# Remainder columns stored through a shared output slot, and a lone quad interleaved with the next pair, in a one-core QKV projection

## The chip, the cores and the metric

The kernel runs on one core of one Trainium2 chip. The metric is the device time of one execution in microseconds (us). The core has five engines with an instruction queue each: TensorE (PE in the profile; its weight loads are PEld), VectorE (DVE), ScalarE (ACT), GpSimd (POOL) and SyncE (SP), which here only issues DMAs. ACT issues some DMAs as well.

## The reference: what is computed

```
x: (16, 512, 768) float32      w_qkv: (768, 2304) float32
qkv = matmul(x, w_qkv)
q, k, v = qkv[..., :768], qkv[..., 768:1536], qkv[..., 1536:]
return stack([q, k, v], axis=0)
```

It is one product of an 8192 x 768 matrix with a 768 x 2304 matrix; its columns are stored as three matrices.

## The kernel before

**Tiles.** The 8192 rows are worked on in 32 pairs of 128 rows, `p` = 0 to 31. The 2304 columns are two blocks of 1024, called `q` = 0 and 1, and a remainder of 256 columns between them. One *quad* is one pair of rows with one block of columns: four output tiles c11, c12, c21, c22 of 128 x 512, held in one SBUF tile `o` (pool `o_pool`, five slots) and stored by two DMAs of 768 KB and 256 KB (`store_quad`, L259/L260 for block 0, L263/L264 for block 1).

**The product.** From pair 2 on a quad is computed with seven products in place of eight (the Strassen-Winograd scheme): `do(u, n)` for n = 1 to 7. Each product is three matmuls of 128x128 by 128x512 (L218). do(1) and do(2) use the bf16 copy `xb` of x and the bf16 block `b1`; the others use sums of x (`s`, made by `sums_x`) and sums of w (`t1` to `t4`, made by `sum_w`). Several products add into one PSUM bank, which is copied out in between: do(1) to bank u.x, copied to c11 by ACT (L232); do(2) to bank u.z, added to c11 by DVE (L236); do(6) adds to u.x, which ACT copies to c12 (L239); do(5) starts bank u.y; do(7) adds to u.x; do(4) adds to u.x, copied to c21 (L249); do(3) adds to u.y, which DVE adds to c12 (L252). A product that adds to a bank has to wait for the copy that reads it. [...]

**The remainder.** `rem(p)` makes the 256 remainder columns of a pair: twelve bf16 matmuls (L268), a copy by ACT (L278) and one store of 256 KB (L279).

**The first three pairs.** While weights are still being loaded, pairs 0 and 1 are computed plainly in bf16 (`block`, L405, copies L395). The order of the program, which is also each engine's order, is: block 0's first half for pairs 0 and 1; `rem(0)` and `rem(1)`, whose stores ACT issues; block 0's second half; the first products of pair 2's first quad, `alone(u, ...)` at L479, with the copies of the last block results (`late[2]`, `late[3]`) and `rem(2)` put between its steps; the casts of the second block's weights on ACT (`cast_js`, L483); block 1's first half for pairs 0 and 1; pair 2's do(4) and the store of its first quad (L495, L496); block 1's second half; pair 2's second quad, `alone(u, {})` at L506.

**The loop.** From pair 3 on, `two(a, b, early)` works both quads of a pair in the order of L283 to L300. `early` transposes the next pair's x on DVE (L134), casts it and sums it on POOL (L176, L185 to L189), and issues the load of the pair after that, half by SP and half by ACT (L126). For pair 3 alone, `early` first ends pair 2's second quad with do(4) and its store.

**What sets the order.** The schedule is manual: every engine executes its instructions in the order of the program, and a wait of one holds all behind it on that engine. SP's and ACT's DMAs are queues of their own (q1 and q10 in the profile). DMAs share eight completion semaphores in turn, so an issue can wait until the DMA eight places earlier has landed. A new `o` tile takes the slot that has been free for longest, and its first writer, the c11 copy at L232 or the copy at L395, waits until the stores of the slot's last tile have landed. The first `o` slot is taken by the staged remainder weights (`str`).

Of the kernel before, what the change touches and what calls it, by code (L numbers as in the profile page):

```python
# [10 lines left out]
def kernel(  # L11
# [20 lines left out]
    nc = tc.nc  # L32
    P = 128
    G = 32
    B, T, H = x.shape
# [3 lines left out]
    KT = K // P  # L39
    KH = KT // 2  # L40
    KC = K // 4
    NP = M // (2 * P)
    CB = 512
    REM = N3 - 4 * CB
    Q_OFF = (0, 2 * CB + REM)
    R_OFF = 2 * CB
    fp32 = mybir.dt.float32
    f32r = mybir.dt.float32r
    bf16 = mybir.dt.bfloat16
    ident = mybir.ActivationFunctionType.Identity  # L50
# [11 lines left out]
    o_pool = ctx.enter_context(tc.tile_pool(name="o", bufs=5))  # L62
    st_pool = ctx.enter_context(tc.tile_pool(name="st", bufs=4))
    or_pool = ctx.enter_context(tc.tile_pool(name="or", bufs=2))
# [13 lines left out]
    b1 = [w_pool.tile([P, KT, CB], bf16, name=f"b1_{q}") for q in range(2)]  # L78
# [12 lines left out]
    stage = {}  # L91
# [108 lines left out]
    def quad(p, q):  # L200
        u = Quad()
        u.p, u.q = p, q
        u.o = o_pool.tile([P, 2, 2 * CB], fp32, name="o", tag="o")
        u.x = u.y = u.z = None
        return u

    def product(u, n, ps, start):
        t1, t2, t3, t4 = ts[u.q]
        if n <= 2:
            h = (n - 1) * KH  # L210
            lhs = [xb[u.p][:, h + j, :P] for j in range(KH)]
            rhs = [b1[u.q][:, h + j, :] for j in range(KH)]
        else:
            k, t = {3: (4, b22[u.q][:]), 4: (0, t4), 5: (1, t1), 6: (2, t2), 7: (3, t3)}[n]
            lhs = [sr[u.p][:, k, j, :] for j in range(KH)]
            rhs = [t[:, j, :] for j in range(KH)]
        for j in range(KH):
            nc.tensor.matmul(  # L218
                ps[:], lhs[j], rhs[j],
                start=(start and j == 0), stop=(j == KH - 1), skip_group_check=True,  # L220
            )

    def bank():
        return ps_pool.tile([P, CB], fp32, name="ps")

    def do(u, n):
        c11, c12 = u.o[:, 0, :CB], u.o[:, 0, CB:]
        c21, c22 = u.o[:, 1, :CB], u.o[:, 1, CB:]
        if n == 1:
            u.x = bank()  # L230
            product(u, 1, u.x, True)
            nc.scalar.activation(c11, u.x[:], ident)  # L232
        elif n == 2:
            u.z = bank()
            product(u, 2, u.z, True)
            nc.vector.tensor_tensor(c11, c11, u.z[:], op=add)  # L236
        elif n == 6:
            product(u, 6, u.x, False)
            nc.scalar.activation(c12, u.x[:], ident)  # L239
        elif n == 5:  # L240
            u.y = bank()
            product(u, 5, u.y, True)
        elif n == 7:
            product(u, 7, u.x, False)
            nc.scalar.activation(c22, u.x[:], ident)  # L245
            nc.vector.tensor_tensor(c22, c22, u.y[:], op=add)  # L246
        elif n == 4:
            product(u, 4, u.x, False)
            nc.scalar.activation(c21, u.x[:], ident)  # L249
        elif n == 3:  # L250
            product(u, 3, u.y, False)
            nc.vector.tensor_tensor(c12, c12, u.y[:], op=add)  # L252

    def rows_of(s, p, lo, hi):
        return out_flat[s, p * 2 * P:(p + 1) * 2 * P, lo:hi].rearrange("(r m) n -> m r n", m=P)

    def store_quad(u):
        if u.q == 0:
            nc.sync.dma_start(rows_of(0, u.p, 0, H), u.o[:, :, :H])  # L259
            nc.sync.dma_start(rows_of(1, u.p, 0, 2 * CB - H), u.o[:, :, H:])  # L260
        else:
            part = 2 * H - Q_OFF[1]
            nc.sync.dma_start(rows_of(1, u.p, H - part, H), u.o[:, :, :part])  # L263
            nc.sync.dma_start(rows_of(2, u.p, 0, H), u.o[:, :, part:])  # L264

    def rem_row(p, r, ps):
        for j in range(KT):
            nc.tensor.matmul(  # L268
                ps, xb[p][:, j, r * P:(r + 1) * P], w_rem[j // KH][:, j % KH, :],
                start=(j == 0), stop=(j == KT - 1), skip_group_check=True,  # L270
            )

    def rem(p, eng=nc.sync):
        ps = ps_pool.tile([P, 2, REM], fp32, name="ps")
        for r in range(2):
            rem_row(p, r, ps[:, r, :])
        o = or_pool.tile([P, 2, REM], fp32, name="orem")
        nc.scalar.activation(o[:], ps[:], ident)  # L278
        eng.dma_start(rows_of(1, p, R_OFF - H, R_OFF - H + REM), o[:])  # L279

    def two(a, b, early):

        do(a, 1)  # L283
        do(b, 1)
        early()
        rem(a.p)
        do(a, 2)
        do(b, 2)
        do(a, 6)
        do(b, 6)  # L290
        do(a, 5)
        do(a, 7)
        do(b, 5)
        do(b, 7)
        do(a, 4)
        do(a, 3)
        store_quad(a)
        do(b, 4)
        do(b, 3)
        store_quad(b)  # L300

    def store_cols(u, r, lo, hi, eng):

        c = Q_OFF[u.q] + lo
        end = Q_OFF[u.q] + hi
        while c < end:
            n = min(end, (c // H + 1) * H)
            row = (2 * u.p + r) * P
            eng.dma_start(  # L309
                out_flat[c // H, row:row + P, c % H:c % H + n - c],  # L310
                u.o[:, r, c - Q_OFF[u.q]:n - Q_OFF[u.q]],
            )
            c = n

    def last(a, b):

        p = a.p

        def rem_stored(r):
            ps = bank()  # L320
            rem_row(p, r, ps[:, :REM])
            o = or_pool.tile([P, 2, REM], fp32, name="orem")
            nc.scalar.activation(o[:, 0, :], ps[:, :REM], ident)  # L323
            row = (2 * p + r) * P
            nc.scalar.dma_start(out_flat[1, row:row + P, R_OFF - H:R_OFF - H + REM], o[:, 0, :])  # L325

        do(a, 1)
        do(b, 1)
        do(a, 2)
        do(a, 6)  # L330
        do(b, 2)
        do(b, 6)
        for u in (a, b):
            store_cols(u, 0, 0, CB, nc.sync)
        for u in (a, b):
            do(u, 5)
            do(u, 7)
            store_cols(u, 1, CB, 2 * CB, nc.sync)
        do(a, 4)
        store_cols(a, 1, 0, CB, nc.scalar)  # L340
        rem_stored(0)
        do(b, 4)
        store_cols(b, 1, 0, CB, nc.scalar)
        for u in (a, b):
            do(u, 3)
            store_cols(u, 0, CB, 2 * CB, nc.sync)
        rem_stored(1)


    ND = 2  # L350
# [18 lines left out]
        for _ in range(n):  # L369
            nc.tensor.matmul(ps[:], zero[:, :P], zero[:], start=True, stop=True)  # L370

    act, dve = nc.scalar, nc.vector

    def cast(q, h, c, w, eng):

        dst = w[:, h * KH:(h + 1) * KH, :]
        if eng is act:
            eng.activation(dst, stage[q, h, c], ident)
        else:
            eng.tensor_copy(out=dst, in_=stage[q, h, c])  # L380
# [35 lines left out]
    def halves(tiles):  # L416
        return [(range(h * KH, (h + 1) * KH), tiles) for h in range(2)]

    def alone(u, after):


        c22 = u.o[:, 1, CB:]
        for n in (1, 2):
            do(u, n)
            after.get(n, lambda: None)()
        do(u, 6)
        do(u, 5)
        act.activation(c22, u.y[:], ident)  # L428
        after.get(5, lambda: None)()
        product(u, 7, u.x, False)  # L430
        dve.tensor_tensor(c22, c22, u.x[:], op=add)
        do(u, 3)

    def ahead(p):
        transpose(p)
        round_x(p)
        sums_x(p)
# [17 lines left out]

    for f in block(0, 0, b1[0], singles):
        f()
    rem(0, act)
    rem(1, act)
    cast(0, 0, 1, bt0, dve)  # L460
    cast(0, 1, 1, bt0, act)
    sum_w(0, 1)
# [4 lines left out]
    late = block(0, 1, bt0, halves(range(4)))  # L467
# [7 lines left out]
    sum_w(0, 3)  # L475
    sums[3](dve)
    sums[4](dve)
    u = quad(2, 0)
    alone(u, {1: late[2], 2: lambda: rem(2), 5: late[3]})  # L479

    def cast_js(q, c, w):
        for j in range(KT):
            act.activation(w[:, j, :], stage[q, j // KH, c][:, j % KH, :], ident)  # L483

    cast_js(1, 0, b1[1])
    bt1 = bt_pool.tile([P, KT, CB], bf16, name="bt")
    cast_js(1, 1, bt1)
    sum_w(0, 4)
    load_x(4, nc.sync)
    t_1 = [tq_pool.tile([P, 2, KH, CB], f32r, name=f"t_1{n}", tag="tq") for n in range(2)]  # L490
# [12 lines left out]
    for f in block(1, 1, bt1, halves(range(4))):  # L503
        f()
    u = quad(2, 1)
    alone(u, {})  # L506

    for p in range(ND + 1, NP):
        def early():
            if p == ND + 1:  # L510
                do(u, 4)
                store_quad(u)
            if p + 1 < NP:
                ahead(p + 1)
            if p + 2 < NP:
                load_x(p + 2, nc.scalar)

        if p < NP - 1:
            two(quad(p, 0), quad(p, 1), early)
        else:  # L520
            last(quad(p, 0), quad(p, 1))


# [28 lines left out]
```

## Time and profile before

| what | value |
|---|---|
| median of three runs | 362.6 us (362.59, 362.60, 363.93) |
| the profiled execution: time | 363.91 us |
| its span, first to last instruction | 362.1 us |
| PE matmul, busy | 352.1 us (97%) |
| PE weight load / DVE / ACT / POOL, busy | 251.2 / 227.7 / 188.7 / 174.3 us |
| moved by DMA | 108.08 MB, 298 GB/s over the span |
| same from 5 to 45 us, in stretches of 5 us | 312 to 406 GB/s, engines' share 1.04 to 1.09 |

The time of an execution holds 1.8 us that lie outside the span. Each of the sixteen DMA engines can have packets of more than one transfer in work, so their share can be over 1. A line of the timeline gives the start of a group of like instructions, its duration, engine, source line, operation, what it writes and reads, how many there are, and in brackets how long the engine had been idle before, and who ended that. A matmul of 128x512 starts every 0.216 us in bf16 and every 0.227 us in the wider type when nothing holds it up, though each is shown with some 0.38 us since they are pipelined. Some records of matmuls are missing.

### The profile page before, as it was taken

The page shows a single profiled execution, that of the slowest core. Times are in us where ns is not written, and L with a number is a line of the kernel's source. Part 1 is how long each engine was busy: PE and PEld are TensorE (multiplying, and loading weights), DVE is VectorE, ACT ScalarE, POOL GpSimd, SP SyncE. Part 2 cuts the span into 40 slices and gives each one's busy share as a digit, 9 for nine tenths or more (in the row PEclk, how much of TensorE's full clock was granted, in tenths as well). Part 3 has the DMA queues.
Part 4 walks back from the last instruction along what each step waited for, and adds up shares of the span by engine and source line. Part 5 has one row for each costly group of instructions (what it writes and reads, how often), then busy time and mean ns, then how long its engine had stood idle before and what let it go on. Part 6 is the DMA issues. An engine that isn't in the chain of part 4 may idle for free.

```text
span 362.1 us, 5215 instructions
## 1 busy us (share of the span) xinstructions
PE 352.1 (97%) x1747; PEld 251.2 (69%) x1779; DVE 227.7 (63%) x240; ACT 188.7 (52%) x317; POOL 174.3 (48%) x181
## 2 busy tenths in 40 slices
PE   8979999999999999999999999999999999999995
PEld 3545577777777777777777777777777777777763
DVE  3679866755656755566765566675565676556643
ACT  4579745455454554454545454545445455545452
POOL 0000773456654446654446664445665444666420
PEclk9999999999999999999999999999999999999999
DMA  7999988989999989899999999898999998989766
GB/s 297 375 376 358 369 285 291 269 286 293 316 306 290 291 277 292 287 319 296 300 272 296 274 325 313 282 276 295 279 308 309 291 289 279 293 281 323 288 248 245
DMA packets 81433, 108.08 MB, mean 298 GB/s; under 512 B 4864, under 2 KB 61440, under 8 KB 81408
## 3 DMA queue, kind: packets, MB, share of 16 engines
q1 hardware_dynamic: 65456, 95.83, 81.2%
q10 hardware_dynamic: 15952, 11.93, 10.0%
q8 instruction: 14, 0.23, 0.3%
q14 instruction: 11, 0.09, 0.1%
HBM read 32.24 MB, written 75.50 MB: 298 GB/s over the span
## 4 chain that ended last, share of the span: by engine, by line
PE 87%; DMA 7%; ACT 4%; issue 1%; ACTq 0%; DVE 0%
PE ps L218 76%; PE ps L268 11%; DMA xin<-in_x_dram 4%; DMA str<-in_w_qkv_dram 2%; DMA out_dram<-o 1%; ACT bt L483 1%; ACT b L483 1%; ACT o L395 1%; ACT o L249 0%; DVE xf L134 0%; ACTq L309 0%; ACT xb L470 0%; ACT orem L323 0%; ACT o L232 0%; ACTq L325 0%
## 5 line engine op out<-in xcount | busy, mean ns | idle before, releaser
L218 PE MATMUL ps<-t,s 128*128 128x512 f32 x720 | 181.1, 399 | 0.2
L218 PEld LDWEIGHTS ps<-t,s 128*128 128x128 f32 x720 | 134.9, 188 | 32.1 <-ACT o L239 0.9
L176 POOL CAST xb<-xf 128x1536 bf16<-128x1536 f32 x29 | 43.8, 1512 | 145.5 <-DVE xf L134 145.5
L246 DVE TENSOR_TENSOR o<-o,ps 128x512 f32<-128x512 f32 x58 | 39.9, 688 | 93.5 <-ACT o L245 93.5
L134 DVE STREAM_TRANSPOSE xf<-xin 128x1536 f32<-128x1536 f32 (+1 forms) x31 | 88.4, 2856 | 2.3 <-DMA xin<-in_x_dram 2.3
L218 PE MATMUL ps<-b,xb 128*128 128x512 bf16 x331 | 81.2, 379 | 3.8 <-ACT xb L470 1.8
L218 PEld LDWEIGHTS <-xb 128*128 128x128 bf16 x360 | 32.7, 98 | 39.3 <-issue 7.9
L239 ACT ACTIVATE o<-ps 128x512 f32<-128x512 f32 x60 | 36.0, 600 | 43.7 <-PE ps L218 40.9
L245 ACT ACTIVATE o<-ps 128x512 f32<-128x512 f32 x58 | 34.7, 599 | 44.3 <-PE ps L218 44.3
L252 DVE TENSOR_TENSOR o<-o,ps 128x512 f32<-128x512 f32 x60 | 41.3, 688 | 21.4 <-PE ps L218 20.2
L218 PE MATMUL ps<-b,s 128*128 128x512 f32 x180 | 50.3, 389 | 0.0
L232 ACT ACTIVATE o<-ps 128x512 f32<-128x512 f32 x60 | 35.8, 597 | 25.6 <-DVE o L252 21.4
L249 ACT ACTIVATE o<-ps 128x512 f32<-128x512 f32 x60 | 35.9, 598 | 24.2 <-PE ps L218 21.3
L268 PE MATMUL ps<-w_rem,xb 128*128 128x256 bf16 x384 | 47.2, 273 | 0.0
L268 PEld LDWEIGHTS <-xb 128*128 128x128 bf16 x384 | 37.3, 98 | 11.3 <-issue 0.8
L236 DVE TENSOR_TENSOR o<-o,ps 128x512 f32<-128x512 f32 x60 | 37.9, 673 | 2.4 <-ACT o L232 1.3
L218 PEld LDWEIGHTS ps<-b,s 128*128 128x128 f32 x180 | 33.7, 188 | 7.2 <-ACT o L428 0.2
L185 POOL TENSOR_TENSOR s<-xf 128x384 fp32r<-128x384 f32 x29 | 30.9, 1067 | 0.0
L186 POOL TENSOR_TENSOR s<-s,xf 128x384 fp32r<-128x384 f32 x29 | 29.4, 1015 | 2.3
L187 POOL TENSOR_TENSOR s<-xf 128x384 fp32r<-128x384 f32 x29 | 29.5, 1018 | 0.0
L189 POOL TENSOR_TENSOR s<-xf,s 128x384 fp32r<-128x384 f32 x29 | 29.4, 1015 | 0.0
L278 ACT ACTIVATE orem<-ps 128x512 f32<-128x512 f32 x31 | 18.5, 598 | 20.2 <-PE ps L268 20.2
(42 smaller groups left out, 113.5 us busy)
## 6 DMA issues: line engine op xcount, KB each, us to landing
out_dram<-o SPq DMA_DIRECT2D x62, 768.0 KB, 5.8
out_dram<-o SPq DMA_DIRECT2D x65, 256.0 KB, 4.3
xin<-in_x_dram SPq DMA_DIRECT2D x66, 192.0 KB, 6.9
xin<-in_x_dram ACTq DMA_DIRECT2D x54, 192.0 KB, 4.4
out_dram<-orem SPq DMA_DIRECT2D x29, 256.0 KB, 5.9
st<-in_w_qkv_dram SPq DMA_DIRECT2D x6, 768.0 KB, 9.2
xin<-in_x_dram SPq DMA_DIRECT2D x2, 768.0 KB, 5.0
st<-in_w_qkv_dram SPq DMA_DIRECT2D x6, 256.0 KB, 6.0
```

What stands on the lines that cost most here:

```text
L134: nc.vector.transpose(turned[:, g:g + n], rows[:, g:g + n])
L176: nc.gpsimd.tensor_copy(out=xb[p][:], in_=xf[p][:])
L185: 1: lambda g: g.tensor_tensor(s[:, 1], a21, a22, op=add),
L218: nc.tensor.matmul(ps[:], lhs[j], rhs[j], start=(start and j == 0), stop=(j == KH - 1), skip_group_check=True,)
L232: nc.scalar.activation(c11, u.x[:], ident)
L236: nc.vector.tensor_tensor(c11, c11, u.z[:], op=add)
L239: nc.scalar.activation(c12, u.x[:], ident)
L245: nc.scalar.activation(c22, u.x[:], ident)
L246: nc.vector.tensor_tensor(c22, c22, u.y[:], op=add)
L249: nc.scalar.activation(c21, u.x[:], ident)
L252: nc.vector.tensor_tensor(c12, c12, u.y[:], op=add)
L268: nc.tensor.matmul(ps, xb[p][:, j, r * P:(r + 1) * P], w_rem[j // KH][:, j % KH, :], start=(j == 0), stop=(j == KT - 1), skip_group_check= ...
```

## The change

It has three parts.

1. `rem` no longer issues its store; it returns a function that does, always on SP. The remainder columns of pairs 0 and 1 are written to one new tile `o_rem` from the pool of output slots, and their two stores are issued on SP behind do(2) and `rem(2)` of pair 2's first quad, ahead of pair 2's own remainder store.
2. `alone` begins with do(6): do(1) and do(2) are written ahead of it by its caller. In pair 2's first quad, the first two of the six casts of `b1[1]` now stand in front of the copy `late[3]`, and `late[3]` still stands behind the copy of c22.
3. Pair 2's second quad does only do(1) and do(2) before the loop; its do(6), do(5), do(7) and do(3) stand behind do(a, 1) and do(b, 1) of pair 3, and its do(4) and store behind pair 3's remainder.

```diff
-    def rem(p, eng=nc.sync):
+    def rem(p, o=None):
         ps = ps_pool.tile([P, 2, REM], fp32, name="ps")
         for r in range(2):
             rem_row(p, r, ps[:, r, :])
-        o = or_pool.tile([P, 2, REM], fp32, name="orem")
-        nc.scalar.activation(o[:], ps[:], ident)
-        eng.dma_start(rows_of(1, p, R_OFF - H, R_OFF - H + REM), o[:])
-
-    def two(a, b, early):
+        if o is None:
+            o = or_pool.tile([P, 2, REM], fp32, name="orem")[:]
+        act.activation(o, ps[:], ident)
+        return lambda: nc.sync.dma_start(rows_of(1, p, R_OFF - H, R_OFF - H + REM), o)
+
+    def two(a, b, early, before=None, after=None):
 
         do(a, 1)
         do(b, 1)
+        if before is not None:
+            before()
         early()
-        rem(a.p)
+        rem(a.p)()
+        if after is not None:
+            after()
         do(a, 2)
...
         c22 = u.o[:, 1, CB:]
-        for n in (1, 2):
-            do(u, n)
-            after.get(n, lambda: None)()
         do(u, 6)
         do(u, 5)
         act.activation(c22, u.y[:], ident)
-        after.get(5, lambda: None)()
+        after()
         product(u, 7, u.x, False)
         dve.tensor_tensor(c22, c22, u.x[:], op=add)
         do(u, 3)
...
-    rem(0, act)
-    rem(1, act)
+    o_rem = o_pool.tile([P, 2, 2, REM], fp32, name="orem2", tag="o")
+    store_rem = [rem(p, o_rem[:, p]) for p in range(2)]
...
+    def cast_j(q, c, w, j):
+        act.activation(w[:, j, :], stage[q, j // KH, c][:, j % KH, :], ident)
+
     u = quad(2, 0)
-    alone(u, {1: late[2], 2: lambda: rem(2), 5: late[3]})
-
-    def cast_js(q, c, w):
-        for j in range(KT):
-            act.activation(w[:, j, :], stage[q, j // KH, c][:, j % KH, :], ident)
-
-    cast_js(1, 0, b1[1])
+    do(u, 1)
+    late[2]()
+    do(u, 2)
+    store = rem(2)
+    store_rem[0]()
+    store_rem[1]()
+    store()
+
+    def between():
+        cast_j(1, 0, b1[1], 0)
+        cast_j(1, 0, b1[1], 1)
+        late[3]()
+
+    alone(u, between)
+    for j in range(2, KT):
+        cast_j(1, 0, b1[1], j)
     bt1 = bt_pool.tile([P, KT, CB], bf16, name="bt")
-    cast_js(1, 1, bt1)
+    for j in range(KT):
+        cast_j(1, 1, bt1, j)
...
     u = quad(2, 1)
-    alone(u, {})
+    do(u, 1)
+    do(u, 2)
 
     for p in range(ND + 1, NP):
         def early():
-            if p == ND + 1:
-                do(u, 4)
-                store_quad(u)
             if p + 1 < NP:
                 ahead(p + 1)
             if p + 2 < NP:
                 load_x(p + 2, nc.scalar)
 
-        if p < NP - 1:
-            two(quad(p, 0), quad(p, 1), early)
+        def fourth():
+            do(u, 4)
+            store_quad(u)
+
+        a, b = quad(p, 0), quad(p, 1)
+        if p == ND + 1:
+            two(a, b, early, lambda: alone(u, lambda: None), fourth)
+        elif p < NP - 1:
+            two(a, b, early)
         else:
-            last(quad(p, 0), quad(p, 1))
+            last(a, b)
```

More of the change, by code (lines that the diff above doesn't have):

```diff
@@ L264, in store_quad @@
             nc.sync.dma_start(rows_of(2, u.p, 0, H), u.o[:, :, part:])
+    act, dve = nc.scalar, nc.vector
     def rem_row(p, r, ps):
@@ L370, in busy @@
             nc.tensor.matmul(ps[:], zero[:, :P], zero[:], start=True, stop=True)
-    act, dve = nc.scalar, nc.vector
     def cast(q, h, c, w, eng):
```

## The prediction, made before the changed kernel ran

> **What bounds the kernel now.** I read the page first: PE is busy for 352.1 of 362.1 us, so only the 10 us in which it isn't can be won. Then the chain of work: from 57 us on it is PE alone, one pair of quads every 10.74 us. No edit touches that loop, so whatever the change does to the moment at which the loop is entered goes to the end one to one. I take as that moment the first matmul of do(a, 2) of pair 3, at 48.92 us; behind it both kernels issue the same instructions in the same order.
>
> Third, the timeline between 21 and 24 us, start of PE's longest wait (columns: start us, duration us, engine, line):
>
> ```profile
> 21.50 2.99 DVE L134 STREAM_TRANSPOSE xf<-xin 128x768 f32<-128x768 f32 x2 [2.31 <-DMA xin<-in_x_dram]
> 23.09 0.84 ACT L470 ACTIVATE xb<-xf 128x768 bf16<-128x768 f32 x1 [1.80 <-DVE xf L134]
> ...
> 23.98 1.47 PE L218 MATMUL ps<-b,xb 128*128 128x512 bf16 x6 [1.76 <-ACT xb L470]
> ```
>
> PE waits for ACT, ACT for DVE, DVE for the load of x pair 2, landed at 21.48. So this stretch is a matter of DMA. Fourth, the DMA queues in two stretches, 16.2 to 20.2 us and 20.5 to 26.5 us (queue: packets, MB, share of 16 engines):
>
> ```profile
> q1 hardware_dynamic: 1224, 1.14, 108.1%
> q8 instruction: 1, 0.02, 2.0%
> ```
>
> ```profile
> q1 hardware_dynamic: 962, 1.88, 81.2%
> q10 hardware_dynamic: 544, 0.52, 24.8%
> ```
>
> q1 is SP's queue, q10 ACT's. The engines are full in both. Though ACT issues the two remainder stores at 16.20 and 17.51, q10 has no packet at all in the first stretch; they move in the second, when the load of x is done on 15 of 16 engines (its landing marks: fifteen from 19.31 to 20.14, the last 21.48). The late one fits the single 16 KB instruction packet of q8, which the trace has from 19.16 for 1.28 us.
>
> Fifth, ACT's and PE's timelines around the third pair's second quad:
>
> ```profile
> 41.80 0.60 ACT L232 ACTIVATE o<-ps 128x512 f32<-128x512 f32 x1
> 43.45 0.60 ACT L239 ACTIVATE o<-ps 128x512 f32<-128x512 f32 x1 [1.05 <-PE ps L218]
> 44.15 0.60 ACT L428 ACTIVATE o<-ps 128x512 f32<-128x512 f32 x1
> 46.49 1.25 ACT L232 ACTIVATE o<-ps 128x512 f32<-128x512 f32 x2 [1.75 <-PE ps L218]
> ```
>
> ```profile
> 42.45 2.61 PE L218 MATMUL ps<-t,s 128*128 128x512 f32 x9
> 44.90 0.84 PE L218 MATMUL ps<-b,s 128*128 128x512 f32 x3
> 45.81 1.24 PE L218 MATMUL ps<-b,xb 128*128 128x512 bf16 x5
> 46.70 1.05 PE L218 MATMUL ps<-t,s 128*128 128x512 f32 x3
> ```
>
> The two copies from 46.49 (L232) are pair 3's c11 of a and b. The second must wait until its output slot is free. The slot was the third pair's first quad's: the wait of that copy names the semaphores of exactly that quad's two stores. Those are (start us, duration; then KB, us to landing):
>
> ```profile
> 37.96 0.40 SPq L259 DMA_DIRECT2D out_dram<-o  x1
> 38.41 0.47 SPq L260 DMA_DIRECT2D out_dram<-o  x1
> ```
>
> ```profile
> out_dram<-o SPq DMA_DIRECT2D x1, 256.0 KB, 6.0
> ```
>
> They land at 43.72 and 38.41 + 5.97 = 44.38 us. Before the change the copy comes at 47.14, so this store has 2.8 us to spare.
>
> **The change, part by part.**
>
> *Remainder stores.* The two DMA issues leave ACT (0.44 and 0.39 us at L279) and come to SP, three in a row behind the first quad's do(2). ACT's cast of bt could start 0.46 us earlier (17.48 instead of 17.94), which frees PE of a 0.2 us hole at 19.3; PE then stands for x at 23.98 anyway, so this is worth 0. For the load of x itself I take 0 as well: no q10 packet ran before it was through on fifteen engines. The other bound is the full 0.5 MB at 395 GB/s, 1.3 us earlier. SP doesn't stand for them: their copies end at 17.5, and pair 2's at 27.4, before SP comes there (28.57). On SP's queue the stores pass pair 2's loads, all weight loads and the load of x 3, which land up to 1.3 us earlier; none of these is waited for (the last weights land at 31.94 and ACT casts them from 33.84). They stand now before the store of the second output quad, the load of x 4 and the third pair's first store. Before, they went ahead of those too, on q10: the bytes ahead of the third pair's store are unchanged. With q1 at full share from 33 to 42 us I take its landing as unchanged, 44.38; ends: 43.28, when its landing marks are complete on fifteen engines, and 45.66, if the two stores cost 1.28 us more behind one another in one queue than beside it. The slot taken by the shared tile costs nothing: it is an unused one; the second pair's output then waits for the first quad's store (landing 36.33, less 1.3) with its copy at 36.36.
>
> [...]
>
> *Copies moved.* Two casts of b1 now precede the copy of the last block result on ACT. Before, PE's first matmul of the next block waits for the first cast: expected at 29.67 (29.44 + 0.23), it starts at 29.85. With the cast at 28.69 instead of 29.16 that 0.18 goes. The late copy frees a bank that is taken only in a later block (the block at 35.72 starts without waiting for the copy of u.x at 37.31, so banks come from those longest free), so it costs 0.
>
> *Interleaving.* All of pair 3's do(1) now stands between do(2) and do(6) of the lone quad. New times, from 40.91 - 0.18 = 40.73: twelve bf16 matmuls at 0.216, 2.59, to 43.32; there is no wait for c11's copy (before 0.25: 42.45 against 42.20). do(6) and do(5) take 1.49 (42.45 to 43.94), to 44.81. do(7) needs c12's copy: last matmul of do(6) at 43.89, copy 0.43 later at 44.32, matmul 0.65 after that (43.45 to 44.10), 44.97; it still waits 0.16. do(7) and do(3) take 1.49, to 46.46; the remainder 12 x 0.109 = 1.31, to 47.77; do(4) 0.70, to 48.47. Against 48.92: 0.45 us won, if nothing else waits.
>
> *The wait it brings.* b's first copy is now wanted 0.40 after its last matmul at 43.10, 43.50 us, but its slot is free at 44.38; ACT starts some 0.04 later (DVE started 0.02 after x had landed), at 44.42. Behind it on ACT, in order, stand c12's copy (0.50 later, as ready copies and casts follow each other by 0.48 to 0.52 from 31 to 37 us: 44.92 instead of 44.32) and c22's; PE's do(7) waits for the former. That adds 0.60: 48.47 + 0.60 = 49.07, or 0.15 us later than before. On SP, the lone quad's store now comes behind the load of x 5 and pair 3's remainder store; its slot is needed again only two pairs later. DVE's transpose of x 4 moves back by about 1.5 us; its product was ready at 51 us for matmuls at 57.29 and has the room. Pair 3's do(1) needs x 3's cast on POOL, done at 41.57 - 0.18 against a need at 42.03: 0.6 us left.
>
> **The sum** for the profiled execution: 363.91 us (span 362.1 and 1.8 around it) + 0.15 = 364.1. Of the three runs shown two are at 362.6 and one at 363.93, and the profiled one is like the last. The steps of 1.3 us fit the load of x landing at 20.2 instead of 21.48. In such an execution before, PE enters the loop at about 47.6. After, it can't: the store's place in a full DMA queue is fixed, so ACT is held to 44.42 and PE to 49.07 just the same. So I expect 364.1 in both, against the median 0.4% more.
>
> **Rivals.**
> 1. *The gate is open.* The store lands by 43.3 to 43.5, as on the fifteen engines. Then the whole 0.45 is won in an execution like the profiled one, 363.5, and one like the median goes from 362.6 to between 362.15 and 363.5. For: only one engine is late. Against: that engine is late through every transfer from 21 to 49 us.
> 2. *The gate is later, and the kernel slower.* One place: the same copy of b. If the stores in one queue with the loads delay the third pair's store by their own 1.28 us, ACT stands till 45.70 and PE enters at 50.35, 365.3 us. It decides from a landing of 44.7 on (364.4 us). For: two queues at once were at 398 GB/s from 20 to 25 us, one alone at 347 from 35 to 40. Against: the slow stretch has 768-byte packets of x, and landings add up without a gap.
> 3. *The change does what it seems meant for.* x lands 1.3 us earlier because the stores are gone, and the gate is open too: 363.91 - 0.45 - 1.3 = 362.15, and from the median 360.85. Against: q10 is empty at that time.
>
> **Chances.** Forecast 0.45, rivals 0.30, 0.18, 0.07. A measurement of this kernel tells about 0.5%, 1.8 us, from no change. Faster than 360.8: 0.07; slower than 364.4: rival 2, 0.18; the rest, 0.75, within. The range goes from 362.1 (rivals 1 and 3 in part) to 364.9, halfway into rival 2.
>
> **What would show it.** In the profile after: the load of x still ends PE's wait near 24.0; six plus six bf16 matmuls from 40.7 with no gap behind them; ACT idle before the second L232 copy until a DMA out_dram<-o lands near 44.4, and PE idle for 0.6 to 2 us before do(7). Wrong is the forecast if that copy starts within 0.5 us of its matmuls, if x is transposed before 21, or if PE waits for POOL's cast ahead of pair 3.

## The result, and the profile after

The changed kernel takes 364.82 us (median of 14 executions, 364.19 to 367.28), the kernel before 363.69 (14 executions, 362.59 to 363.93). The ratio, here and below taken over the executions and not from the medians, is 1.0049, 95% interval 1.0033 to 1.0066. It is slower, by 1.1 us between the medians. The profiled execution of the changed kernel took 366.13 us with a span of 364.3.

With more executions the times before are seen to lie in two groups: six of the 14 at 362.6 to 362.7 and eight at 363.7 to 363.9, so that the profiled one (363.91) is of the usual kind. The changed kernel has no execution under 364.19. Eight of its 14 end by 364.83 with a granted clock of 0.998 to 1.0, six at 365.1 to 367.3 with 0.994 to 0.995.

The timeline from 20 to 23 us, the place of PE's longest wait before (the second line is cut off by the window):

```profile
20.29 3.01 DVE L134 STREAM_TRANSPOSE xf<-xin 128x768 f32<-128x768 f32 x2 [1.09 <-DMA xin<-in_x_dram]
...
22.79 0.39 PE L218 MATMUL ps<-b,xb 128*128 128x512 bf16 x1 [0.66 <-ACT xb L472]
```

In this execution the load of x 2 landed at 20.16, not 21.48, and PE began 1.19 us earlier (22.79 for 23.98). So x is early in this execution, and late in the one profiled before; the two groups of times before are these two cases. What became of that is seen on ACT from 40 us on:

```profile
41.76 0.60 ACT L232 ACTIVATE o<-ps 128x512 f32<-128x512 f32 x1 [0.75 <-PE ps L218]
44.84 0.60 ACT L232 ACTIVATE o<-ps 128x512 f32<-128x512 f32 x1 [2.48 <-DMA out_dram<-o]
44.93 4.85 ACTq L126 DMA_DIRECT2D xin<-in_x_dram  x1
45.34 0.59 ACT L239 ACTIVATE o<-ps 128x512 f32<-128x512 f32 x1
```

These are pair 3's first copies of a and b, the load of x 5, and c12 of the lone quad. The second copy stood 2.48 us for a store. The DMA issues show which: the 256 KB store issued at 37.21 landed 7.2 us later, at 44.43 (38.41 and 44.38 before).

```profile
out_dram<-o SPq DMA_DIRECT2D x1, 256.0 KB, 7.2
```

PE, in the same stretch:

```profile
39.57 2.75 PE L218 MATMUL ps<-b,xb 128*128 128x512 bf16 x12
41.97 1.74 PE L218 MATMUL ps<-t,s 128*128 128x512 f32 x6
45.98 0.97 PE L218 MATMUL ps<-t,s 128*128 128x512 f32 x3 [2.27 <-ACT o L239]
46.79 1.33 PE L218 MATMUL ps<-b,s 128*128 128x512 f32 x3
47.93 2.68 PE L270 MATMUL ps<-w_rem,xb 128*128 128x256 bf16 x12
50.36 0.93 PE L218 MATMUL ps<-t,s 128*128 128x512 f32 x3
51.13 1.47 PE L218 MATMUL ps<-b,xb 128*128 128x512 bf16 x6
```

The twelve matmuls of the lone quad's do(1) and do(2) and of pair 3's two do(1) follow each other without a gap, as does do(6) behind them. Then do(7) waits 2.27 us for c12's copy. And a second thing is new: the twelve remainder matmuls take 2.68 us from first to last, against 1.49 before, one every 0.213 us instead of 0.109. The windows table says why (columns: stretch, its length, busy time and count of five engines, granted clock, DMA share, GB/s):

```profile
44.00:47.00 3.00, 1.02 (x4) 0.87 (x5) 0.00 (x0) 1.57 (x3) 2.28 (x3) 0.99 1.04 408
47.00:50.00 3.00, 3.00 (x13) 1.85 (x12) 2.53 (x3) 0.00 (x0) 0.00 (x0) 0.50 0.77 246
```

The granted clock is 0.50 from 47 to 50 us; the trace's own record has it halved from 46.95 for 3.41 us. The loop is entered, by the mark of the prediction, at 51.13 instead of 48.92: 2.21 us later, and the span is 2.2 us longer. Against the kernel before with x early, which enters at 47.78 (see the instruction packet below), it is 3.35 us.

### The profile page after: what moved, and what is told of

It reads as the page before. It is cut to its first block, busy times and chain, and to the rows that moved or that the text cites. A ratio compares the mean times of both kernels' runs of the same rounds, so it can differ in the third digit from the quotient of the medians.

```text
span 364.3 us, 5241 instructions
## 1 busy us (share of the span) xinstructions
PE 355.5 (98%) x1779; PEld 252.1 (69%) x1779; DVE 227.6 (62%) x240; ACT 188.2 (52%) x317; POOL 174.2 (48%) x181
## 4 chain that ended last, share of the span: by engine, by line
PE 86%; DMA 6%; ACT 3%; SPq 1%; ACTq 1%; issue 1%; DVE 0%; DVEq 0%
PE ps L218 76%; PE ps L270 11%; DMA xin<-in_x_dram 2%; DMA out_dram<-o 2%; DMA st<-in_w_qkv_dram 2%; ACT b L481 1%; ACT bt L481 1%; SPq L126 1%; ACT o L400 1%; ACT o L249 0%; DVE xf L134 0%; ACTq L316 0%; SPq L142 0%; ACT xb L472 0%; ACT orem L330 0%
## 5 line engine op out<-in xcount | busy, mean ns | idle before, releaser
L176 POOL CAST xb<-xf 128x1536 bf16<-128x1536 f32 x29 | 43.8, 1512 | 149.0 <-DVE xf L134 149.0
L218 PE MATMUL ps<-b,xb 128*128 128x512 bf16 x360 | 87.7, 380 | 0.7 <-ACT xb L472 0.7
L218 PEld LDWEIGHTS <-xb 128*128 128x128 bf16 x360 | 32.7, 98 | 38.4 <-issue 7.9
L270 PE MATMUL ps<-w_rem,xb 128*128 128x256 bf16 x384 | 48.4, 277 | 0.0
```

What stands on the lines that cost most here:

```text
L176: nc.gpsimd.tensor_copy(out=xb[p][:], in_=xf[p][:])
L218: nc.tensor.matmul(ps[:], lhs[j], rhs[j], start=(start and j == 0), stop=(j == KH - 1), skip_group_check=True,)
L270: nc.tensor.matmul(ps, xb[p][:, j, r * P:(r + 1) * P], w_rem[j // KH][:, j % KH, :], start=(j == 0), stop=(j == KT - 1), skip_group_check= ...
```

## The experiments

The theory (G) is that the store gate and the clock after it make the whole loss. The rivals are the stores, the interleaving as such, and causes of the half clock other than PE's idle time. Separately, two theories are tried on when x lands: F, that the 16 KB instruction packet sets it; S, that ACT's stores do.

### Part 1 alone

```diff
     u = quad(2, 1)
     do(u, 1)
     do(u, 2)
+    alone(u, lambda: None)
...
-        cast_j(1, 0, b1[1], 0)
-        cast_j(1, 0, b1[1], 1)
         late[3]()
...
-            two(a, b, early, lambda: alone(u, lambda: None), fourth)
+            two(a, b, early)
```

(The lone quad's do(4) and store go back into `early`, all casts behind `late[3]`.)

> Part 1 alone: the two remainder stores on SP through the shared output slot; casts and the lone quad as before. Theory G (the changed kernel is late because the second c11 copy of pair 3 waits for the third pair's store, landing at 44.4 us, and PE's clock halves after the 2.3 us that PE stands still for it): no such wait here, since that copy comes at 46 to 47 us again; so no time over 363.9 us, and a granted clock of 0.998 or more. On the load of x there are two theories. S (ACT's stores held it up): x lands at 20.2 in every execution and the time is 362.5 us each time. F (the 16 KB instruction packet holds up one DMA engine, and it is chance whether x is still on it): a mixture as before, some executions at 362.5 and some at 363.7, median between.

Measured: 363.90 us against 363.78, ratio 1.0003 (0.9989 to 1.0018). One of twelve executions at 362.8, ten at 363.6 to 364.1 and one at 365.4 (clock 0.994). In the profiled one x landed at 21.34. S falls: ACT issues no store here, and x is late as often as before or oftener. The one execution over 364.1 wasn't foreseen; the kernel before has one like it among its 32 (365.75, clock 0.994). In the profiled one PE stands 2.00 us for x (21.94 to 23.94).

### Part 3 alone

```diff
-    o_rem = o_pool.tile([P, 2, 2, REM], fp32, name="orem2", tag="o")
-    store_rem = [rem(p, o_rem[:, p]) for p in range(2)]
+    rem(0, eng=act)()
+    rem(1, eng=act)()
...
-        cast_j(1, 0, b1[1], 0)
-        cast_j(1, 0, b1[1], 1)
         late[3]()
```

(Shortened: `rem` takes `eng` again, the two calls of `store_rem` go, and all casts stand behind `late[3]`.)

> Part 3 alone: lone quad interleaved with pair 3; ACT issues the remainder stores early and casts stand as before. Theory G: the copy waits for the store landing at 44.4 us, PE enters the loop at 49.1 to 49.6, so 364.2 to 364.7 us, and more where the clock halves (only where x came early and PE stood still for over 2 us). Rival (the stores behind one another on SP are what makes the kernel late): no loss, 363.2 to 363.7 us.

Measured: 364.42 us, ratio 1.0029 (1.0012 to 1.0047): seven executions at 364.08 to 364.45, five at 365.80 to 366.08 with a clock of 0.995. Part 3 alone makes the loss, as G has it. The profiled one has the half clock; PE's timeline shows the same two marks, at the same place:

```profile
45.78 0.96 PE L218 MATMUL ps<-t,s 128*128 128x512 f32 x3 [1.99 <-ACT o L239]
46.58 1.26 PE L218 MATMUL ps<-b,s 128*128 128x512 f32 x3
47.65 2.76 PE L270 MATMUL ps<-w_rem,xb 128*128 128x256 bf16 x12
```

### The gate opened: b starts behind the lone quad

```diff
         do(a, 1)
-        do(b, 1)
         if before is not None:
             before()
+        do(b, 1)
         early()
```

> The changed kernel, but pair 3's b starts (its do(1)) behind the lone quad, and only a's do(1) stands in front of it. Theory G: the copy of b into the late slot is then wanted at about 46 us with x early, after the store's landing at 44.4, so no wait and no clock drop; do(6) of the lone quad stays covered by a's do(1). PE enters the loop 0.2 to 0.4 us earlier than in the kernel with the stores alone: 362.0 to 362.4 us with x early, 363.3 with x late. Rival (the interleaving itself or the stores cost the time): 364.4 us or more, as in the changed kernel.

Measured: 362.71 us, ratio 0.9983 (0.9962 to 1.0004): six executions at 362.05 to 362.25, four at 363.17 to 363.44, and two at 364.9 and 365.2 with a clock of 0.994 to 0.995, which weren't foreseen. The copy of b no longer waits for a store:

```profile
45.31 0.60 ACT L232 ACTIVATE o<-ps 128x512 f32<-128x512 f32 x1 [1.76 <-DVE o L252]
```

The slot's store lands at 44.41 there. One line of code takes the loss away and leaves the cover of do(6).

### The wait filled with matmuls

```diff
+    def busy_w(n):
+        ps = bank()
+        for _ in range(n):
+            nc.tensor.matmul(ps[:], b1[1][:, 0, :P], b1[1][:, 1, :], start=True, stop=True)
...
-            two(a, b, early, lambda: alone(u, lambda: None), fourth)
+            two(a, b, early, lambda: alone(u, lambda: busy_w(9)), fourth)
```

> The changed kernel with nine matmuls of 128x512 added (their result is not used) in front of do(7) of the lone quad, 1.94 us of work in the time in which PE waits for the copy. Theory G: the wait stays and the entry to the loop stays at 49.5, but PE isn't idle for longer than 0.5 us, so the clock stays at 1.0 in every execution: 364.3 to 364.7 us, none above 365. Rival (the half clock has a cause other than the idle time, or the loss of up to 2 us in some executions has nothing to do with the clock): the spread from 364.2 to 367.3 stays, or the nine matmuls come on top, 366 us and more.

Measured: 365.04 us, five executions at 364.5 to 365.0 and four at 366.35 to 366.8, three of those with a clock of 0.993 to 0.995. The profiled one (364.76) keeps its clock: PE stands 0.54 us and the remainder takes 1.48. But the upper group was not expected. In an execution with x late PE stands 1.8 to 2.0 us at 22 us as well, where nothing fills it (1.76 in the kernel before, 2.00 with part 1 alone); whether those were such executions no trace shows. So x had to be made early first.

### The instruction packet moved

```diff
-    busy(4)
+    busy(2)
```

Two of PE's fifteen warm-up matmuls go; the result doesn't use them.

> The kernel before with one edit: two of its fifteen warm-up matmuls (their result isn't used) are left out, so PE comes to each place of its program two matmuls (0.43 us) of the first block earlier in instructions, later in work: the 16 KB instruction packet of 19.2 us is asked for 0.43 us later in PE's work. Theory F (the packet falls between the third and the fourth part of the load of x, and then x lands 1.2 us late): at 19.6 us the fourth part is already under way, so x lands at 20.2 in all executions, 362.5 to 362.9 us each. Rival (x is late by chance of the DMA engines or because of ACT's stores): the two clusters at 362.65 and 363.8 us stay with most executions in the later.

Measured: twelve executions from 362.41 to 362.77, median 362.55, while the kernel before on the same chip had 13 at 362.5 to 362.9, ten at 363.7 to 363.9 and two at 365.6. The late group is gone, as F has it. The DMA queues from 19 to 20.5 us, before and then with the two matmuls left out:

```profile
q1 hardware_dynamic: 256, 0.48, 99.5%
q8 instruction: 1, 0.02, 5.3%
```

```profile
q1 hardware_dynamic: 262, 0.50, 103.8%
```

The packet has left the stretch; it starts at 20.63, when x has landed (20.28). The last landing mark of the weight load behind x, for which nobody waits, comes 1.4 us behind the others (23.61 against 22.18), but so it does in the kernel before (23.81 against 22.17): one of its sixteen marks is late in both, and only x's last mark differs (20.28 against 21.48). The packet's start alone doesn't decide that: with part 3 alone it starts at 19.15, as before (19.16), and x lands at 20.19. The packet moved further than the 0.43 us expected, by 1.47, which stays unexplained.

> The changed kernel with the same two warm-up matmuls left out. Theory G with F: x always early, the copy of b still waits for the store at 44.4, PE always stands for 2.3 us: no execution under 364.1; those in which the clock stays up 364.2 to 364.8, those in which it halves for 3.4 us (granted clock 0.995) 365.8 to 366.2. Rival (the early x is worth its 1.2 us in the changed kernel too): about 363.2 us.

Measured: 366.15 us, ratio 1.0071 (1.0047 to 1.0095): two executions at 364.44 and 364.55, four at 366.09 to 366.78 with a clock of 0.994 to 0.995. The early x is worth nothing in the changed kernel. The profiled one is of the first two, the changed kernel without the half clock:

```profile
46.04 0.96 PE L218 MATMUL ps<-t,s 128*128 128x512 f32 x3 [2.37 <-ACT o L239]
46.84 0.85 PE L218 MATMUL ps<-b,s 128*128 128x512 f32 x3
47.53 1.49 PE L270 MATMUL ps<-w_rem,xb 128*128 128x256 bf16 x12
48.77 0.95 PE L218 MATMUL ps<-t,s 128*128 128x512 f32 x3
49.56 1.47 PE L218 MATMUL ps<-b,xb 128*128 128x512 bf16 x6
```

From do(7) to the entry it needs 3.52 us (46.04 to 49.56), the changed kernel's first profile 5.15 (45.98 to 51.13). The half clock costs 1.63 us between these two profiles.

> The changed kernel without those two warm-up matmuls and with eleven matmuls (result not used, 2.4 us) in the wait ahead of do(7). With x early PE now stands nowhere for over 0.7 us before the loop. Theory G: no execution has a granted clock under 0.997 and all lie from 364.2 to 364.8 us. Rival (the half clock doesn't come from PE's idle time): about half of the executions have 0.995 and lie at 366 us.

(`busy_w(11)`.) Measured: eight executions, none with a clock under 0.997, seven at 364.37 to 364.90; the eighth, 365.51, is the profiled one and shows another wait, 1.1 us of PE for POOL's cast of x 3 (see the end). With the same gate and the wait ahead of do(7) filled, the half clock is in none of eight; with the wait (2.37 us in the profiled one) a mean clock of 0.994 to 0.995 is in four of six: it comes from PE's standing still.

> The kernel with only a's do(1) in front of the lone quad, without those two warm-up matmuls. Theory G with F: no wait for the store, x always early: 362.0 to 362.3 us in every execution, 0.4% under the kernel before. Rival: the clusters at 363.2 and 365 us stay.

Measured: 362.19 us, ratio 0.9978 (0.9964 to 0.9992), ten of twelve at 362.06 to 362.45, two at 363.5 and 364.0. It beats both kernels, as expected but for those two.

### The single parts, with x always early

> Part 1 alone (remainder stores on SP through the shared slot), without the two warm-up matmuls, so that x is always early. By the prediction's step the stores were not in the way of anything: the same as the kernel before without those two matmuls, 362.4 to 362.7 us. Rival (their DMA issues on ACT, 0.83 us, or the later weights cost something): 362.0 us or less.

> Parts 1 and 2 (stores, and two casts ahead of the last block copy), lone quad whole before the loop, without the two warm-up matmuls. By the prediction the casts are worth 0.18 us: 0.1 to 0.25 us less than part 1 alone, 362.3 to 362.5 us, and PE goes from do(3) of the first quad to the next block without its gap of 0.18. Rival (the copy put behind them holds up a bank): no less than part 1 alone.

> Only a's do(1) in front of the rest of the lone quad; stores early on ACT and casts as before; without the two warm-up matmuls. By the prediction this is worth the covered wait of do(6), 0.25 us, and brings no wait for a slot: 362.2 to 362.4 us, PE without a gap between do(1), do(2) and do(6). Rival (the gain of the best kernel needs the stores moved): 362.5 us or more.

Measured, in this order (before, on the same chip: 363.67): 363.46, 363.45 and 362.20 us, ratios 1.0004 (0.9989 to 1.0018), 1.0005 (0.9993 to 1.0016) and 0.9967 (0.9955 to 0.9980). The third, with only a's do(1) moved and the stores left on ACT, has the time expected; it isn't told apart from the kernel with the gate open and x early (362.19). PE without a gap was expected too, but its one profile is its slowest execution (363.24, the other nine end by 362.29), in which PE stands 0.96 us for POOL's cast of x 3. The first is a miss by 0.9 us against 362.55 for the kernel before with x early; two of its ten executions are at 362.6. The second misses its range by as much. The second shows the casts' effect on PE: do(3) of the first quad to the next block takes 0.71 us (27.68 to 28.39) instead of 0.84 (27.72 to 28.56) in the first; but the time is the same. Both lose time in the same place, on ACT, here in the kernel with the stores alone:

```profile
46.47 4.01 ACTq L126 DMA_DIRECT2D xin<-in_x_dram  x2
50.53 0.60 ACT L281 ACTIVATE orem<-ps 128x512 f32<-128x512 f32 x1 [3.46 <-PE ps L218]
51.02 1.08 ACT L239 ACTIVATE o<-ps 128x512 f32<-128x512 f32 x2
```

ACT is 4.01 us busy with issuing the two halves of its load of x 5, where the kernel before needs 1.35, and 1.96 with x early; the copies behind it come late, and PE stands 0.63 us until 51.76, ahead of pair 3's do(7), which needs the first of the two copies.

### What makes ACT's issue slow

Two theories, each with its own remedy, on top of the first of the three kernels above:

```diff
+    for _ in range(5):
+        nc.scalar.activation(tiny[:], zero[:, :1], ident)
     make_identity(nc, eye)
```

```diff
-    load_rows(1)
+    load_rows(1, nc.scalar)
```

(`load_rows` takes the engine that issues.)

> Part 1 alone without the two warm-up matmuls, and with five small activations of 128 x 1 added on ACT at the start, where ACT is idle. Theory I (ACT's instruction packet): with five instructions more ahead of it the 8 KB packet of q14 comes at 44 to 45 us again, ACT's first issue of the load of x 5 takes under 1 us, PE doesn't stand at 51 us, and the time is 362.5 to 362.7 us. Theory D (first DMA of ACT): the issue still takes 2 to 4 us, 363.2 to 363.9.

> Part 1 alone without the two warm-up matmuls, and with the second load of x (pair 1) issued by ACT instead of SP at 1 us, so that ACT's queue is used early; ACT has one instruction more, not five. Theory D: the later issue takes under 1 us and the time is 362.5 to 362.9 us. Theory I: the packet comes only some 0.6 us earlier, at 46.9 us, the issue still takes 2 us or more, 363.0 to 363.9.

Measured: 362.64 and 362.61 us, all ten executions of each from 362.54 to 362.79. Both remedies bring the time back to that of the kernel before with x early. In the first, ACT's 8 KB instruction packet (on q14) comes at 43.12 instead of 47.45 and the issue takes 0.90:

```profile
46.58 0.90 ACTq L126 DMA_DIRECT2D xin<-in_x_dram  x2
47.90 0.60 ACT L281 ACTIVATE orem<-ps 128x512 f32<-128x512 f32 x1 [0.73 <-PE ps L270]
```

In the second the packet stays at 47.52, and the issue takes 1.93. So neither theory stands alone. All fifteen profiles sort as follows. In seven the issue is ACT's first DMA and the packet comes after the issue has begun: it takes 3.1 to 6.1 us, and its first half ends 1.6 to 1.9 us after the packet's start (47.45 and 49.33 in the kernel above). In three it is ACT's first DMA but the packet comes before: 0.9 to 2.1 us (2.12 with part 1 alone and x late, where the packet comes at 47.45 and the issue at 47.73). In five ACT has issued a DMA before: 0.9 to 2.0 us, even where the packet comes later. That the issue waits for the packet would fit the ends of the seven first halves, but no run shows such a wait; why an issue behind an earlier DMA of ACT takes no more than 2.0 us stays open as well. In the changed kernel itself the issue takes 6 us (4.85 and 1.18) and costs PE nothing seen: in the execution without the half clock PE's span behind the entry is no longer than that of the best kernels (313.2 us in each).

## Why the prediction was right or wrong

**What bounds the kernel, and the mark at 48.92.** Right: the span moved by what the mark moved, 2.2 us.

**Remainder stores.** Right that they weren't in the way of x (part 1 alone: x late as before) and that the third pair's store would land where it did (44.43 for 44.38). Wrong in one thing: that taking the issues from ACT costs nothing. It costs 0.9 us where x is early (in eight of ten executions), by the slow issue at 46 us; where x is late, the issue comes later, behind the packet, and nothing is lost (363.90 against 363.78).

**The other bound, x 1.3 us earlier** (an estimate from 0.5 MB at 395 GB/s), isn't what came: x is late without ACT's stores too (21.34 with part 1 alone). In the second stretch, from 20.5 to 26.5 us, the two queues do run side by side (q1 81.2%, q10 24.8%).

**Copies moved.** 0.18 us foreseen, 0.13 to 0.15 seen on PE (0.71 us for 0.86 before and 0.84 with the stores alone), with no bank held up.

**Interleaving.** The wait of do(6) is gone; from do(1) to the entry the kernel with a's do(1) alone in front needs 7.65 us (39.42 to 47.07) and the kernel before with x early 8.04 (39.74 to 47.78). The prediction's sum had 0.27 for this (40.73 to 48.47, 7.74, for 8.01 before), 0.39 is won.

**The wait it brings** is the step that failed, and in its price alone. Place, store, landing time and the chain from ACT to PE are as written down. But the sum priced the wait at 0.60 us, put the entry at 49.07 and held PE's later work at its old pace; the entry came at 51.13. Of the 2.06 us between, 0.05 are the landing (44.43 for 44.38), 0.37 are ACT, which starts 0.41 us after the landing (44.43 to 44.84) and not 0.04, and the rest is the half clock, a term that the sum doesn't have. ACT's 0.41 is not a fixed price: it is 0.41 in all four profiles in which ACT waits for this store and has issued no DMA before, and 0.11 with part 3 alone (44.54 to 44.65), where it has. Why stays open.

With x early the prediction foresaw a wait of up to 2 us and held that it costs no more than the shorter one; there it is wrong. PE stands 2.27 us (43.71 to 45.98), and after it the granted clock halves, in the profiled execution for 3.41 us, at a price of 1.63. By their mean clock of 0.994 to 0.995 it was so in 6 of 14 executions (10 of 20 together with the kernel without the two warm-up matmuls). Without the half clock the changed kernel takes 364.2 to 364.8, forecast 364.1; with it 365.1 to 367.3. Of these six, three lie at 365.1 to 365.3 and one at 367.28, less and more than 1.63 explains; no trace shows them.

The length of the wait alone doesn't tell whether the clock halves. With part 3 alone it halved after 1.99 us (the twelve remainder matmuls took 2.76 us, the mean clock was 0.995). It stayed after 2.37 us in the profiled execution of the changed kernel without the two warm-up matmuls (1.00 from 44 to 54 us), and after 2.00 us with part 1 alone and x late (the remainder behind it took 1.47 us). What else decides, these profiles don't show.

**The two clusters before.** Right: they are the load of x at 20.2 and at 21.5, and the late one is gone when the 16 KB packet comes later (20.63 instead of 19.16). Wrong was to compare with 362.6 as the usual time; eight of 14 executions are at 363.7 to 363.9. It was also no good sign of being wrong that x is transposed before 21: it was (20.29), but the kernel before does so too in its early group. Against that, the forecast of 364.1 was close to no change, and the kernel is slower by more than its interval.

**Rivals.** The first (gate open) is what moving b back makes of the kernel. The second was the right side by the wrong mechanism: the store isn't later. The third fell: no x gained by the stores.

## What to carry to other kernels

Before work is pulled forward, look at what its first write needs: here a copy pulled 3.6 us forward (wanted at 43.50 instead of 47.14, by the prediction's sum) met a store that lands at 44.35 to 44.68 in every profile, whether issued at 37 or at 38.4, and everything gained ahead of it was lost at that one wait. Price a wait of TensorE not by its length alone but also by what the clock does after it: here another 1.63 us were lost to the half clock (between two profiles) after 2.27 us of standing still, and it was seen in 10 of 20 executions. And when one kernel's times fall into two groups, find the cause first, since a change of two warm-up matmuls was worth as much as the rest (1.1 us in the late group) and made the later comparisons easier to read.

## What the runs showed of the hardware that had not been expected

- Instruction packets move through the DMA queues beside the data: in the kernel before, the fourteen 16 KB packets of q8 took 0.95 to 1.28 us each, the one at 19.16 being 5.3% of sixteen engines' time from 19 to 20.5 us. Where x was late (part 1 alone and before), fifteen of its sixteen landing marks came by 20.14 and the last 1.2 to 1.3 us later, about that packet's own time (1.28), and DVE's transpose began behind the last mark (21.50 after 21.48 before). It was worth 1.1 us here.
- By a mean clock of 0.994 to 0.995, PE's clock halved in 10 of 20 executions; in the one profiled, it did so after 2.27 us of idle time, for 3.41 us.
- ACT's issue of two 192 KB loads took 0.9 to 6.1 us in the fifteen profiles. It took 3.1 us and more only in the seven where it was ACT's first and ACT's own 8 KB packet (q14) came after it had begun.
- POOL's cast of 128x1536 of x 3 (L176) took 2.85 us before and 2.84 in the changed kernel, and 4.50 to 4.51 in three profiles (with the wait filled and x early, with stores and casts, with a's do(1) alone). In two of the three PE waited 1.0 to 1.1 us for it, the wait that the prediction gave 0.6 us of room.
